# Conv taps released earlier, the local values projected behind the norm sums, compressed scores one head later

## The chip, the cores and the metric

The kernel runs on 1 core of one Trainium2 chip. The metric is the device time of one execution in microseconds (us). The engines are called TensorE (PE), VectorE (DVE), ScalarE (ACT), GpSimd (POOL) and SyncE (SP, which issues the loads). All matrix work is float32: a weight tile is split into a rounded part `hi` and a remainder `lo` by ACT and DVE, and PE makes three products of them.

## The reference, cut to what matters

Two transformer blocks follow each other on 256 tokens of width 1024. The change touches the second one, which computes, from `xn = rms_norm(x)`, three branches and their gated sum:

```python
q_nsa, kv_nsa, g_nsa, conv_in, q_mem, g_merge = split(xn @ w_in)
# branch 1: sparse attention, 8 heads: compressed scores, selected blocks, window
kc = rms_norm(compress_blocks(k_c));  vc = compress_blocks(v_c)
o_nsa = gate0 * softmax(q kc) vc + gate1 * softmax(q ks) vs + gate2 * softmax(q kw) vw
# branch 2: convolution of 31 taps over time, one weight per channel (512 channels)
u = a * sigmoid(ag)
u = silu(layer_norm(depthwise_conv(u, 31) + conv_b))
# branch 3: attention over 256 memory tokens, 4 heads
o_m = softmax(qm km) vm
gm = sigmoid(g_merge)
merged = gm[0] * (o_nsa @ w_nsa_out) + gm[1] * (u @ w_conv_out) + gm[2] * (o_m @ w_mem_out)
h = x + merged @ w_out            # then a gated feed-forward layer
```

## The kernel before, in words

Activations lie transposed: features on the 128 partitions, 256 tokens along the free axis. Weights stream in tiles of 128x1024; `Stream.prepare` issues the load on SP, the cast to `hi` on ACT (line 520) and the subtraction to `lo` on DVE (line 522), with 4 raw buffers and 3 each of `hi` and `lo`. A tile of the gate projection is 8 blocks of 128x128; its matmuls are 8 with `hi` (line 324), 8 with `hi` on the activation's remainder (line 326) and 8 with `lo` (line 328). Two tiles fill one PSUM buffer `pj`, and DVE takes it out into `gm` with line 1082.

Block two runs in these steps. The projection `w2a` makes the conv input `u`, the compressed operands, the heads' queries and keys. Then `compress` (a generator, stepped by `next(cmp)`) makes the compressed keys `kcn` and values, `nsa_operands` (stepped by `next(pre)`) makes the norm sums of queries and keys (line 1311, matmuls with 1 or 2 columns), their inverse roots `hn_y` and the split operands. `nsa` holds the attention: `first(n)` makes the scores of head n on PE, their maxima and the scaling on DVE and the exponentials on ACT; `scores()` makes the compressed scores of all heads, with a chain of 12 DVE steps on the tile `sc`; `turned(n)` transposes the weights of head n, `compressed()` transposes `sc` into `PcT` (line 1386), and `values(i)` multiplies with the values `vsw` and, as its last matmul, with `PcT` (line 1445). Between these steps stand the 24 tiles of the gate projection `w2g`, taken one at a time by `fill(gates, 1)`; they cover the attention's latency. `gemm_a` with `w2v` makes the local values `vsw` (line 367, 48 matmuls, two tiles).

What sets the order: from the heads' projection to the end of the gates PE's order is the written one (`manual_schedule` for PE alone). ACT, DVE and the rest of PE are ordered by a scheduler that takes the ready instruction of the highest priority; each engine then runs its queue strictly in order. Loads' splits and evacuations carry a raised priority. `issue_after(x)` keeps an instruction out of the queue until x stands in it.

The convolution is 4 columns of 31 DVE instructions on 128x256 (`conv_taps`, lines 1531 and 1534), each adding to `cv`. Columns 0 and 1 are free to go as soon as `u` is there. Column 2 is held until `N.marks[4]`, column 3 until `N.marks[7]`, where `N.marks[n]` is the product of gate and denominator of head n (line 1415). After the taps comes `conv_norm`: a fold on DVE (lines 1544, 1545), a mean matmul on PE (line 1549), the subtraction (line 1551), squares on ACT (line 1553), the sum matmul (line 396), an inverse root in small steps on DVE (lines 381 to 387), a transpose on PE that spreads it (line 403), the scaling (line 1560), a SiLU and the split into `uc`. Behind the gates PE runs the three output projections `wmo` (of `om`), `wno` (of `on`) and `wco` (of `uc`), then `wo2` (line 308 first).

Of the kernel before, what the change touches and what calls it, by code (L numbers as in the profile page):

```python
# [13 lines left out]
OP = mybir.AluOpType  # L14
# [423 lines left out]
def fill(steps, n):  # L438
    for _ in range(n):
        next(steps, None)  # L440


def finish(steps):
    for _ in steps:
        pass
# [93 lines left out]
def bc(ap, n, at=1):  # L539

    shape = list(ap.shape)
    shape.insert(at, n)
    return ap.unsqueeze(at).to_broadcast(shape)
# [499 lines left out]
def block_two(K, B, KM, vm, out):  # L1043
    nc, tc, a, par, con = K.nc, K.tc, K.a, K.par, K.con
# [7 lines left out]
    cv = K.t4("cv")  # L1052
    kc2 = [K.small("PT", [128, 384], bufs=4)[:, :256].rearrange("p (g t) -> p g t", g=2) for _ in range(2)]
    N = Bag()
# [3 lines left out]
    ag, u = K.t4("ag"), K.small("u", [128, 4, 286], bufs=1)  # L1058
# [39 lines left out]
    with tc.manual_schedule(engines={mybir.EngineType.PE}):  # L1098
        heads = K.steps_b(_Shift(st, 64), 8, 12, B.X, evb)
        fill(heads, 6)  # L1100
        cmp = compress(K, kc2, N)
        for _ in range(6):
            next(cmp)
            fill(heads, 1)
        next(cmp)
        pn = K.gemm_n(K.narrow("wgn", B.gain), B.x)
        with tc.high_priority(offset=50000):
            nc.vector.tensor_tensor(gn, pn, rr, op=OP.mult)
        next(cmp)
        K.gemm_a(K.stream("w2v", 256), 8, 1, B.X, 256, evv)  # L1110
        next(cmp)
        pre = nsa_operands(K, N, B.eps)
        next(pre)
        pg = K.pt()[:, :48].rearrange("p (t n) -> p t n", t=2)
        for t in range(2):
            mm(pg[:, t], lhsT=gn[:, t * 128:t * 128 + 128], rhs=con["fold"][:, :24], start=True, stop=True)
        N.gate = K.small("gate", [128, 2, 24], bufs=1)
        with tc.issue_after(s3.ins):
            nc.scalar.preload_act_table_set("natural_log_exp_and_others")
            sigmoid(K, N.gate, pg)  # L1120
        gates = K.steps_b(K.stream("w2g"), 8, 24, B.X, evg)
        fill(gates, 2)
        next(cmp)
        finish(pre)
        fill(gates, 1)
        finish(cmp)
        with tc.issue_after(s3.ins):
            last = nsa(K, N, ON, mem_attention(K, N, KM, vm, OM), gates)
        finish(gates)

    conv_taps(K, u, cv, {2: N.marks[4], 3: N.marks[7]})
    with tc.issue_after(last.ins):
        with tc.high_priority(offset=50000):
            UC = conv_norm(K, cv)
# [67 lines left out]
def compress(K, kc2, N):  # L1202

    nc, par, con = K.nc, K.par, K.con
    mm = nc.tensor.matmul
    pos = par["pos"].rearrange("p (k j) -> p k j", k=2)
    pa = K.pt().rearrange("p (k n) -> p k n", k=2)
    h = K.small("cmp_h", [128, 128], bufs=1)
    for kv in range(2):
        sides = []  # L1210
        for half in range(2):
            s = K.small("P0", [128, 2, 128], bufs=4).rearrange("p a (j c) -> p (a j) c", c=32)
            nc.gpsimd.memset(s[:, :, 30:], 0.0)
            with K.tc.high_priority(offset=50000):
                for g in range(2):
                    nc.vector.tensor_tensor(
                        s[:, :, g * 15:g * 15 + 15],
                        kc2[kv][:, g].rearrange("p (i j) -> p j i", j=8)[:, :, half:half + 15],
                        pos[:, kv, 8 * half:8 * half + 8].unsqueeze(2).to_broadcast([128, 8, 15]), op=OP.add)
            sides.append(s)  # L1220
        for ch in range(4):
            for j in range(4 * ch, 4 * ch + 4):
                if j % 2 == 0:
                    raw = K.small("P1", [128, 2, 256], bufs=4)
                    with K.tc.high_priority(offset=100000):
                        nc.sync.dma_start(raw, K.a["wc1"][kv * 4 + ch][:, (j % 4) * 256:(j % 4) * 256 + 512])
                o = 32 * (j % 4)
                mm(pa[o:o + 32, kv], lhsT=sides[j // 8][:, j % 8], rhs=raw[:, j % 2], start=j < 4, stop=j >= 12,
                   skip_group_check=True)
            if 4 * kv + ch < 7:  # L1230
                yield
    part = K.small("P1", [128, 2, 256], bufs=4)
    nc.scalar.copy(part, pa)
    yield
    ph = K.pt()[:, :128].rearrange("p (k m g c) -> p k m g c", k=2, m=2, g=2)
    for kv in range(2):
        for m in range(2):
            mm(ph[:, kv, m, :, :15], lhsT=part[:, kv, m * 128:m * 128 + 128],
               rhs=con["fold"], start=True, stop=True)
    hv = h.rearrange("p (a c) -> p a c", c=16)  # L1240
    phv = ph.rearrange("p k m g c -> p (k m g) c")
    nc.gpsimd.memset(h, 0.0)
    nc.vector.tensor_copy(hv[:, :, :15], phv[:, :, :15])
    t = K.small("cmp_t", [128, 128], bufs=1)
    nc.vector.tensor_tensor(t, h, h, op=OP.mult)
    nc.vector.tensor_scalar(t, t, 0.044715, 1.0, op0=OP.mult, op1=OP.add)
    nc.vector.tensor_tensor(t, t, h, op=OP.mult)
    sigmoid(K, t, t, 2 * (2 / np.pi) ** 0.5)
    nc.vector.tensor_tensor(h, h, t, op=OP.mult)
    yield  # L1250
    h5 = h.rearrange("p (k m c) -> p k m c", k=2, m=2)
    w2 = par["wc2"].rearrange("p (k m d) -> p k m d", k=2, m=2)

    pk = K.pt()[:, :16]
    for g in range(2):
        for m in range(2):
            mm(pk[g * 64:g * 64 + 64], lhsT=w2[:, 0, m], rhs=h5[:, 0, m, g * 16:g * 16 + 16], start=m == 0, stop=m == 1)
    k1, k2 = K.small("cmp_k", [128, 16], bufs=1), K.small("cmp_k2", [128, 16], bufs=1)
    nc.vector.tensor_copy(k1, pk)
    nc.vector.tensor_tensor(k2, k1, k1, op=OP.mult)  # L1260

    pv = K.pt()[:, :64]
    for i in range(4):
        for m in range(2):
            mm(pv[32 * i:32 * i + 32], lhsT=h5[:, 1, m], rhs=w2[:, 1, m], start=m == 0, stop=m == 1)
    N.vcb = K.small("cmp_v", [128, 128], bufs=1)
    nc.vector.tensor_tensor(N.vcb.rearrange("p (g d) -> p g d", g=2), bc(pv, 2),
                            con["slot"].unsqueeze(2).to_broadcast([128, 2, 64]), op=OP.mult)
    yield
    pn = K.pt()[:, :16]  # L1270
    mm(pn, lhsT=con["mean64"], rhs=k2, start=True, stop=True)
    nc.vector.tensor_scalar(k2, pn, EPS, None, op0=OP.add)
    y = rsqrt_exp(K, k2, *(K.small(n, [128, 16], bufs=1) for n in ("cmp_y", "cmp_w")))
    nc.vector.scalar_tensor_tensor(k1, k1, K.gain_k[:, 0:1], y, op0=OP.mult, op1=OP.mult)
    N.kcn = K.small("cmp_kn", [128, 2, 16], bufs=1)
    nc.vector.tensor_tensor(N.kcn, bc(k1, 2), con["half"].unsqueeze(2).to_broadcast([128, 2, 16]), op=OP.mult)


def sigmoid(K, out, x, scale=1.0):
# [66 lines left out]
def nsa(K, N, ON, mem, gates):  # L1346

    nc, par, con = K.nc, K.par, K.con
# [38 lines left out]


    cz = con["causal0"]
    S, N.marks = {}, {}  # L1390

    def first(n):
        i, g = divmod(n, 2)
# [55 lines left out]
    fill(gates, 1)  # L1449
    first(0)  # L1450
    fill(gates, 1)
    scores()
    first(1)
    fill(gates, 1)
    late = []
    for i in range(4):
        turned(2 * i)
        if i < 3:
            first(2 * i + 2)
        else:  # L1460
            late.append(mem(3))
            next(late[-1])
        fill(gates, 1)
        turned(2 * i + 1)
        if i == 0:
            compressed()
        fill(gates, 1)
        if i < 3:
            first(2 * i + 3)
        values(i)  # L1470
        fill(gates, 1)
        if i:
            next(late[-1 - (i == 3)])
        if i < 3:
            late.append(mem(i))
            next(late[-1])
        fill(gates, 1)
        if i:
            finish(late[-2])
        if i < 2:  # L1480
            fill(gates, 1)
# [42 lines left out]
def conv_taps(K, u, cv, behind):  # L1524
    nc, par, con = K.nc, K.par, K.con
    mm = nc.tensor.matmul
    w = par["conv_w"].rearrange("p (c k) -> p c k", c=4)
    for c in range(4):
        with K.tc.issue_after(behind[c].ins) if c in behind else nullcontext():
            o = cv[:, c * 256:c * 256 + 256]  # L1530
            nc.vector.tensor_scalar(o, u[:, c, :256], w[:, c, 0:1], par["conv_b"][:, c:c + 1],
                                    op0=OP.mult, op1=OP.add)
        for k in range(1, 31):
            nc.vector.scalar_tensor_tensor(o, u[:, c, k:k + 256], w[:, c, k:k + 1], o, op0=OP.mult, op1=OP.add)  # L1534
# [71 lines left out]
```

## Time and profile before

| | |
|---|---|
| times of three runs | 929.54, 930.87, 931.36 us (median 930.87) |
| the profiled execution | 931.74 us, of which the span is 929.9 us |
| PE busy | 903.5 us (97% of the span) |
| DVE busy | 680.2 us (73%) |
| ACT busy | 491.6 us (53%) |
| mean granted clock of PE | 0.987 of full speed |
| `lo` splits, DVE, line 522 | 278 of 1224 ns mean |
| conv taps, DVE, line 1534 | 120 of 476 ns mean |
| gate-like matmuls, PE, lines 324, 326, 328 | 280 to 300 ns each, every 120 ns at full clock |

The profile gives for each instruction its start, its duration and what its engine was waiting for. The durations of neighbours overlap (a matmul of 283 ns starts 120 ns after the last one), so costs below are differences of starts. A granted clock of 1.00 is TensorE's level of 2.4 GHz, 0.50 its level of 1.2 GHz. All windows are us from the start of the span; block two's part up to the output projection lies at 480 to 716.

### The profile page before, as it was taken

How to read it: one execution, taken by the hardware profiler on the slowest of the kernel's cores; microseconds unless marked ns; L12 is line 12 of the kernel's file. 1: busy time of each engine (PE TensorE's matmuls, PEld its weight loads, DVE VectorE, ACT ScalarE, POOL GpSimd, SP SyncE). 2: the span in 40 equal slices, each digit the busy share in tenths (PEclk: the TensorE clock that was granted, in tenths of full speed). 3: DMA queues.
4: the chain of work that ended last, by engine and by line, in shares of the span. 5: the costliest groups of instructions: out<-in, count | busy, mean ns of one | idle time of the engine just before them, and what ended most of it. 6: DMA issues, size and time to landing. Idle time of an engine off the chain costs nothing.

```text
span 929.9 us, 17029 instructions
## 1 busy us (share of the span) xinstructions
PE 903.5 (97%) x6818; PEld 831.3 (89%) x6818; DVE 680.2 (73%) x1169; ACT 491.6 (53%) x747; POOL 52.7 (6%) x82
## 2 busy tenths in 40 slices
PE   8998999999999999999999998999979999999998
PEld 6996789999999999888899897899869988888887
DVE  6997768866777665555567968789989788878653
ACT  6654665644556554444435435677734565555432
POOL 1000002200010000011110000000002200000000
PEclk9999999999999999999999979999989999999999
DMA  7644327665755666566655843244335556666662
GB/s 276 195 137 136 98 67 205 221 204 173 222 181 180 181 184 184 166 185 182 184 182 179 262 124 109 74 136 116 112 113 158 184 174 187 183 186 187 195 206 66
DMA packets 45728, 155.64 MB, mean 167 GB/s; under 512 B 5201, under 2 KB 6737, under 8 KB 45649
## 3 DMA queue, kind: packets, MB, share of 16 engines
q1 hardware_dynamic: 45216, 153.48, 54.1%
q8 instruction: 53, 0.87, 0.4%
q10 hardware_dynamic: 432, 1.08, 0.4%
q14 instruction: 27, 0.21, 0.1%
HBM read 153.49 MB, written 1.05 MB: 166 GB/s over the span
## 4 chain that ended last, share of the span: by engine, by line
PE 91%; DVE 5%; ACT 1%; issue 1%; DMA 0%; SPq 0%; DVEq 0%; ACTq 0%
PE pj L295 17%; PE pj L324 16%; PE pj L326 16%; PE pj L328 15%; PE pj L296 9%; PE pj L367 5%; DVE lo L522 2%; PE pj L309 1%; PE pj L310 1%; PE pj L308 1%; ACT hi L520 1%; PE pt L1311 1%; PE pt L913 1%; PE pt L1442 1%; PE pt L403 1%
## 5 line engine op out<-in xcount | busy, mean ns | idle before, releaser
L520 ACT CAST hi<-raw 128x1024 fp32r<-128x1024 f32 (+1 forms) x278 | 288.6, 1041 | 306.9 <-PE pj L326 139.2
L522 DVE TENSOR_TENSOR lo<-raw,hi 128x1024 fp32r<-128x1024 f32 (+1 forms) x278 | 339.8, 1224 | 105.2 <-ACT hi L520 97.2
L295 PE MATMUL pj<-hid,hi 128*128 128x512 f32 x378 | 134.2, 400 | 0.0
L295 PE MATMUL pj<-xf,hi 128*128 128x512 f32 x320 | 113.2, 399 | 0.0
L296 PE MATMUL pj<-hid,lo 128*128 128x256 f32 x378 | 106.2, 281 | 0.0
L296 PE MATMUL pj<-xf,lo 128*128 128x256 f32 x320 | 89.8, 281 | 0.0
L295 PEld LDWEIGHTS pj<-hid,hi 128*128 128x128 f32 x378 | 71.1, 188 | 17.3
L295 PEld LDWEIGHTS pj<-xf,hi 128*128 128x128 f32 x320 | 60.1, 188 | 14.9
L296 PEld LDWEIGHTS pj<-hid,lo 128*128 128x128 f32 x378 | 71.5, 189 | 0.0
L296 PEld LDWEIGHTS pj<-xf,lo 128*128 128x128 f32 x320 | 60.5, 189 | 0.0
L1534 DVE SCALAR_TENSOR_TENSOR cv<-u,par,cv 128x256 f32<-128x256 f32 x120 | 53.8, 476 | 1.2
L324 PE MATMUL pj<-xm,hi 128*128 128x256 f32 x336 | 52.1, 299 | 0.0
L324 PEld LDWEIGHTS pj<-xm,hi 128*128 128x128 f32 x336 | 45.7, 198 | 4.9 <-ACT hi L520 2.5
L326 PE MATMUL pj<-xm,hi 128*128 128x256 f32 x336 | 48.5, 288 | 0.0
L328 PE MATMUL pj<-xm,lo 128*128 128x256 f32 x336 | 47.2, 283 | 0.0
L469 POOL TENSOR_TENSOR acc<-acc,ffr 128x256 f32<-128x256 f32 (+1 forms) x25 | 27.3, 1101 | 310.9 <-ACT ffr L462 288.9
L328 PE MATMUL pj<-xn,lo 128*128 128x256 f32 x304 | 44.8, 286 | 0.0
L326 PEld LDWEIGHTS pj<-xm,hi 128*128 128x128 f32 x336 | 44.7, 198 | 0.0
L326 PE MATMUL pj<-xn,hi 128*128 128x256 f32 x304 | 44.0, 285 | 0.0
L324 PE MATMUL pj<-xn,hi 128*128 128x256 f32 x304 | 43.8, 285 | 0.0
L328 PEld LDWEIGHTS pj<-xm,lo 128*128 128x128 f32 x336 | 43.5, 193 | 0.0
L328 PEld LDWEIGHTS pj<-xn,lo 128*128 128x128 f32 x304 | 39.7, 192 | 0.5 <-issue 0.4
(471 smaller groups left out, 1639.0 us busy)
## 6 DMA issues: line engine op xcount, KB each, us to landing
raw<-in_wf_dram SPq DMA_DIRECT2D x64, 512.0 KB, 3.9
raw<-in_wgu_dram SPq DMA_DIRECT2D x44, 512.0 KB, 3.7
raw<-in_w1g_dram SPq DMA_DIRECT2D x24, 512.0 KB, 3.8
raw<-in_w2g_dram SPq DMA_DIRECT2D x24, 512.0 KB, 3.7
raw<-in_wdn_dram SPq DMA_DIRECT2D x22, 512.0 KB, 3.8
raw<-in_w2a_dram SPq DMA_DIRECT2D x20, 512.0 KB, 4.0
raw<-in_wo_dram SPq DMA_DIRECT2D x16, 512.0 KB, 3.7
raw<-in_w1a_dram SPq DMA_DIRECT2D x14, 512.0 KB, 4.5
```

What stands on the lines that cost most here:

```text
L295: mm(ps, lhsT=st.hi(w), rhs=x.both(k), start=k == 0, stop=False, skip_group_check=True)
L296: mm(ps[:, :T], lhsT=st.lo(w), rhs=x.h(k), start=False, stop=k == kt - 1, skip_group_check=True)
L308: mm(ps[:, j], lhsT=st.hi(w), rhs=x.h(k), start=k + j == 0, stop=False, skip_group_check=True)
L309: mm(ps[:, j], lhsT=st.hi(w), rhs=x.l(k), start=False, stop=False, skip_group_check=True)
L324: mm(ps[:, j], lhsT=st.hi(o + k), rhs=x.h(k), start=k == 0, stop=False)
L326: mm(ps[:, j], lhsT=st.hi(o + k), rhs=x.l(k), start=False, stop=False)
L328: mm(ps[:, j], lhsT=st.lo(o + k), rhs=x.h(k), start=False, stop=k == kt - 1)
L367: mm(pss[t], lhsT=xx(k)[:, t * 128:t * 128 + 128], rhs=ww(o + k), start=k == 0 and xx == x.h and ww == st.hi, stop=k == kt - 1 and ww == s ...
L469: self.engine.tensor_tensor(a, a, s, op=OP.add)
L520: nc.scalar.copy(hi[:, o:o + n], raw[:, o:o + n])
L522: nc.vector.tensor_tensor(lo[:, o:o + n], raw[:, o:o + n], hi[:, o:o + n].bitcast(F32), op=OP.subtract)
L1534: nc.vector.scalar_tensor_tensor(o, u[:, c, k:k + 256], w[:, c, k:k + 1], o, op0=OP.mult, op1=OP.add)
```

## The change

Three edits, all in block two:

1. The first two gate tiles are moved ahead, to where the values' projection stood, and `gemm_a` of `w2v` moves to where these tiles stood: behind the norm sums (line 1311), the transposes of the gate input and the gate's sigmoid, and ahead of the step of `compress` that needs its sigmoid.
2. `scores()` follows `first(1)` and no longer precedes it; and `compressed()` follows the gate tile that it preceded.
3. Column 2 of the conv is held until the compressed keys `kcn` are made, no longer until head 4; column 3 until head 4, no longer until head 7.

```diff
@@ block_two
-        K.gemm_a(K.stream("w2v", 256), 8, 1, B.X, 256, evv)
+        gates = K.steps_b(K.stream("w2g"), 8, 24, B.X, evg)
+        fill(gates, 2)
         next(cmp)
         pre = nsa_operands(K, N, B.eps)
         next(pre)
...
             sigmoid(K, N.gate, pg)
-        gates = K.steps_b(K.stream("w2g"), 8, 24, B.X, evg)
-        fill(gates, 2)
+
+        K.gemm_a(K.stream("w2v", 256), 8, 1, B.X, 256, evv)
         next(cmp)
...
-    conv_taps(K, u, cv, {2: N.marks[4], 3: N.marks[7]})
+    conv_taps(K, u, cv, {2: N.marks["keys"], 3: N.marks[4]})
@@ compress
-    nc.vector.tensor_tensor(N.kcn, bc(k1, 2), con["half"].unsqueeze(2).to_broadcast([128, 2, 16]), op=OP.mult)
+    N.marks = {}
+    N.marks["keys"] = nc.vector.tensor_tensor(N.kcn, bc(k1, 2), con["half"].unsqueeze(2).to_broadcast([128, 2, 16]), op=OP.mult)
@@ nsa
+    first(1)
     scores()
-    first(1)
     fill(gates, 1)
...
         turned(2 * i + 1)
+        fill(gates, 1)
         if i == 0:
             compressed()
-        fill(gates, 1)
```

No instruction's size or count of arithmetic changes. Lines behind the edits stand 1 or 2 lower in the changed file. How the queues move is shown at three places.

DVE, ahead of the inverse root `hn_y` that the compressed step on PE needs (`lo` is a weight tile's remainder, `gm` the evacuation of two gate tiles, `cmp_h` the compressed hidden layer). Before:

```order
L1284 RECIPROCAL gate_6162<-gate_6162 128x48
L522 TENSOR_TENSOR lo_6385<-raw_6382,hi_6384 128x1024
L1082 TENSOR_TENSOR gm_5244<-pj_6168,rr_5366 128x512
L1249 TENSOR_TENSOR cmp_h_5760<-cmp_h_5760,cmp_t_6113 128x128
L1294 SCALAR_TENSOR_TENSOR hn_y_6150<-hn_w_6151,hn_y_6150 128x32
```

and now:

```order
L1286 RECIPROCAL gate_6160<-gate_6160 128x48
L522 TENSOR_TENSOR lo_6385<-raw_6382,hi_6384 128x1024
L1250 TENSOR_TENSOR cmp_h_5760<-cmp_h_5760,cmp_t_6111 128x128
L1296 SCALAR_TENSOR_TENSOR hn_y_6148<-hn_w_6149,hn_y_6148 128x32
L1536 SCALAR_TENSOR_TENSOR cv_5250<-u_5257,par,cv_5250 128x256
```

The evacuation of the first two gate tiles has left this place; it now stands ahead of the norm sums.

DVE, at the end of the taps (`cv` the conv's sum, `ffr` its fold, `on` and `om` the attention outputs, `lo_7665` and later the tiles of `wmo`). Before:

```order
L1534 SCALAR_TENSOR_TENSOR cv_5250<-u_5257,par,cv_5250 128x256 x2
L1150 TENSOR_TENSOR gm_5249<-pj_7757,gm_5249 128x512
L522 TENSOR_TENSOR lo_7826<-raw_7823,hi_7825 128x1024
L1534 SCALAR_TENSOR_TENSOR cv_5250<-u_5257,par,cv_5250 128x256
L1544 TENSOR_TENSOR ffr_7586<-cv_5250 128x512
```

and now:

```order
L522 TENSOR_TENSOR lo_7665<-raw_7662,hi_7664 128x1024
L427 TENSOR_TENSOR on_5241<-pt_7363,on_5241 128x256
L1536 SCALAR_TENSOR_TENSOR cv_5250<-u_5257,par,cv_5250 128x256 x3
L1546 TENSOR_TENSOR ffr_7586<-cv_5250 128x512
L1547 TENSOR_TENSOR ffr_7586<-ffr_7586 128x256
L522 TENSOR_TENSOR lo_7697<-raw_7694,hi_7696 128x1024
L1082 TENSOR_TENSOR gm_5249<-pj_7375,rr_5366 128x512
L522 TENSOR_TENSOR lo_7729<-raw_7726,hi_7728 128x1024
L1553 TENSOR_TENSOR cv_5250<-cv_5250,pt_7587 128x1024
```

The taps end three instructions behind the last heads' `on`, ahead of the last gate evacuation; before, they ended among the evacuations of `wmo`, five weight tiles later.

PE, where the conv norm's inverse root is spread (line 403; `pj_7725` and `pj_7693` are pairs of `wmo`, `pj_7855` the fourth pair in the list `wmo`, `wno`). Before:

```order
L328 MATMUL pj_7855<-on_5241,lo_7859 128x256
L396 MATMUL pt_7596<-con,ffr_7586 128x1 x2
L328 MATMUL pj_7855<-on_5241,lo_7859 128x256
L403 MATMUL pt_7617<-con,rs_y_7604 128x128 x2
L324 MATMUL pj_7693<-om_5242,hi_7696 128x256 x2
```

and now:

```order
L326 MATMUL pj_7725<-om_5242,hi_7728 128x256 x2
L326 MATMUL pj_7725<-om_5243,hi_7728 128x256 x2
L328 MATMUL pj_7725<-om_5242,lo_7729 128x256 x2
L403 MATMUL pt_7617<-con,rs_y_7604 128x128 x2
L324 MATMUL pj_7693<-om_5242,hi_7696 128x256 x2
```

Between the sum (line 396) and the spreading (line 403) stood one matmul; now 33 of `wmo` stand there. The mean matmul (line 1549, now 1551) has moved from among `wno` to right behind the first memory-value product of the last head pair, ahead of all of `wmo`.

## Rows read from the trace of the kernel before

**Rows 1.** The page: the chain that ended last, shares of the span by engine.

```profile
PE 91%; DVE 5%; ACT 1%; issue 1%; DMA 0%; SPq 0%; DVEq 0%; ACTq 0%
```

**Rows 2.** Stretches: length, busy PE, PEld, DVE, ACT, POOL, granted clock, DMA share, GB/s.

```profile
547.00:553.00 6.00, 6.00 (x32) 6.00 (x31) 0.00 (x0) 0.00 (x0) 0.00 (x0) 0.53 0.31 87
561.40:564.00 2.60, 0.05 (x1) 0.00 (x0) 2.21 (x6) 0.18 (x1) 0.00 (x0) 1.00 0.48 172
564.00:568.40 4.40, 4.34 (x48) 3.84 (x49) 3.06 (x11) 0.41 (x1) 0.00 (x0) 0.61 0.43 123
577.00:579.20 2.20, 0.17 (x3) 0.03 (x1) 2.20 (x9) 0.88 (x2) 0.00 (x0) 1.00 0.50 188
581.00:585.30 4.30, 4.30 (x24) 4.12 (x24) 3.46 (x18) 0.94 (x3) 0.00 (x0) 0.60 0.12 48
579.40:598.90 19.50, 18.32 (x132) 16.14 (x131) 14.17 (x57) 13.88 (x38) 0.00 (x0) 0.91 0.29 82
598.90:615.00 16.10, 16.10 (x131) 15.86 (x131) 10.60 (x33) 12.17 (x31) 0.00 (x0) 1.00 0.44 132
615.00:665.00 50.00, 50.00 (x399) 46.12 (x398) 48.38 (x130) 37.67 (x79) 0.00 (x0) 1.00 0.41 118
665.00:715.60 50.60, 42.59 (x311) 40.46 (x311) 44.92 (x76) 20.12 (x28) 8.69 (x4) 0.93 0.39 124
686.80:691.80 5.00, 0.00 (x0) 0.00 (x0) 4.62 (x14) 0.14 (x1) 2.08 (x1) 0.89 0.35 126
691.80:697.40 5.60, 5.59 (x26) 5.60 (x27) 4.04 (x9) 3.05 (x6) 0.00 (x0) 0.50 0.00 0
```

**Rows 3.** Waits, 530 to 720: who waited for whom, total us, times, longest.

```profile
PE pt L403 <- DVE rs_y L387: 5.0, 1, 5.0
...
PE pt L1257 <- DVE hn_y L1294: 2.6, 1, 2.6
...
PE pt L1364 <- DVE cmp_kn L1276: 2.0, 1, 2.0
```

**Rows 4.** Timeline of DVE behind the norm sums: start, us, instruction.

```profile
561.89 1.22 DVE L522 TENSOR_TENSOR lo<-raw,hi 128x1024 fp32r<-128x1024 f32 x1 [0.40 <-ACT hi L520]
563.04 0.68 DVE L1082 TENSOR_TENSOR gm<-pj,rr 128x512 f32<-128x512 f32 x1
563.64 0.28 DVE L1249 TENSOR_TENSOR cmp_h<-cmp_h,cmp_t 128x128 f32<-128x128 f32 x1
563.84 0.18 DVE L1294 SCALAR_TENSOR_TENSOR hn_y<-hn_w,hn_y 128x32 f32<-128x32 f32 x1
```

**Rows 5.** Timeline of DVE at the compressed scores.

```profile
578.93 0.19 DVE L1276 TENSOR_TENSOR cmp_kn<-cmp_k,con 128x32 f32<-128x32 f32 x1
...
593.39 0.42 DVE L1386 COPY PcT<-pt 128x256 f32<-128x256 f32 x1 [0.30 <-PE pt L1385]
```

**Rows 6.** Timeline of PE at the compressed scores.

```profile
580.97 1.23 PE L1398 MATMUL pt<-ks,qs 128*128 128x256 f32 x4
...
598.31 0.69 PE L1445 MATMUL pt<-PcT,cmp_v 32*128 32x256 f32 x2
```

**Rows 7.** Timeline of DVE at the last conv taps.

```profile
659.43 0.42 DVE L427 TENSOR_TENSOR on<-pt,on 128x256 fp32r<-128x256 f32 x1
659.76 2.56 DVE L1534 SCALAR_TENSOR_TENSOR cv<-u,par,cv 128x256 f32<-128x256 f32 x5
...
679.22 0.48 DVE L1534 SCALAR_TENSOR_TENSOR cv<-u,par,cv 128x256 f32<-128x256 f32 x1
```

**Rows 8.** Timeline of PE from the last gates to the output projection.

```profile
665.07 1.03 PE L1518 MATMUL pt<-PTm,vm 128*128 128x256 f32 x4
...
681.01 0.70 PE L1549 MATMUL pt<-ffr,con 128*128 128x256 f32 x2
...
691.81 0.69 PE L403 MATMUL pt<-con,rs_y 128*128 128x128 f32 x2 [5.03 <-DVE rs_y L387]
...
715.58 0.28 PE L308 MATMUL pj<-mrg,hi 128*128 128x256 f32 x1
```

More of the change, by code (lines that the diff above doesn't have):

```diff
@@ L1389, in nsa @@
     cz = con["causal0"]
-    S, N.marks = {}, {}
+    S = {}
     def first(n):
```

## The prediction

> **What bounds the kernel now.** I read the page first. Its chain of waits gives PE 91% and DVE 5% [rows 1], and the table gives PE 97% busy: the time is PE's queue, and it shortens where PE waits or runs at half clock. The stretches show where that is in block two [rows 2]. From 598.9 to 665 PE is busy 66.1 of 66.1 us at a granted clock of 1.00; nothing is to be had there. The losses lie at three places, and the list of waits names their releasers [rows 3]:
>
> - 561.4 to 564.0: PE is busy 0.05 us; it waits 2.6 us for `hn_y`. Then 4.4 us run at a clock of 0.61.
> - 577.0 to 579.2: busy 0.17 us; it waits 2.0 us for `cmp_kn`, the tile of `kcn`. From 581.0 to 585.3 the clock is 0.60.
> - 665 to 715.6: busy 42.59 of 50.60 us, so 8.0 us idle, 5.0 of them at line 403 for `rs_y`. Behind it 5.6 us run at 0.50, which costs 5.6 x 0.50 = 2.8 us. Together 10.8 us.
>
> **Edit 1, the gate tiles ahead of the norm sums.** PE's work is only swapped: `gemm_a` and the two gate tiles have 48 matmuls each, 0.12 us apart. What shortens the wait for `hn_y` is DVE's queue. Before `hn_y` stand there the split `lo` (561.89), `gm` (563.04), `cmp_h` (563.64) and `hn_y` itself (563.84) [rows 4]. The evacuation `gm` leaves this place, as the order shows: 563.64 - 563.04 = 0.60 us. What starts DVE's run there, the cast on ACT that `lo` waits for (0.40 us), is as it was, and it gives 0 or 0.40. So the gain is 0 (if `hn_y`'s own chain through ACT ends last) to 1.0, and up to 1.4 with a little of the 4.4 us at 0.61 back. I take 0.8: the evacuation is a direct row, the rest a fraction. The loads of the two weights change places in SP's queue and are of the same size; four raw buffers let them be issued ahead, so I count nothing for them. If that cover were gone, a tile late by its split would cost one `lo`, 1.22 us.
>
> On the half clock behind the two waits, a row and a rule part. From 547 to 553 PE is busy 6.00 of 6.00 us, without a wait, and is granted 0.53 [rows 2]: matmuls of one and two columns keep the clock down there by themselves. The Trainium skill, "TensorE: Matmul & The Clock Gate", section "Loop structure matters more than you think", says that the loop nest decides whether matmuls stay warm, and that waits between them send the clock down. By that rule the half clock behind each of the two waits would go with the wait; by the row it may stay. I let most of it stay.
>
> **Edit 2, scores one head later.** The 4 matmuls of a head's scores are busy 1.23 us at the nearest row [rows 6], and the last one's end overlaps what follows, so that I count 1.0. They now stand ahead of the wait for `kcn` and fill 1.0 of its 2.0 us. That is the gain, unless the head's queries are late themselves (0). If the wait's end also spares half clock, 4.3 x 0.40 = 1.7 us come on top: 0 to 2.7.
>
> The same edit has a price. `scores()` brings 12 DVE steps on `sc`, which end in the copy to `PcT`. Before, they run at once; now the reductions of head 1 and a few taps that edit 3 sets free come first. From `cmp_kn` (578.93) to the copy (593.39) it was 14.5 us [rows 5], in a window where DVE is busy 14.17 of 19.5 us [rows 2]. The foreign work ahead of it is now about 6 taps (6 x 0.51 = 3.1 us) and the head's reductions (some 1.5), of which part falls into the 5.3 idle us: I estimate 16 us, so the copy ends at about 595.4 if `cmp_kn` comes as before. The first reader on PE is line 1445 at 598.31 [rows 6], 2.9 us later. A front gain of 2.2 leaves 0.7 of that, so PE does not wait, or by up to 2 us. I take 1.4 for edit 2: the 1.0, and 0.4 of the half clock. Bounds: -1 (all cover gone) to 2.7. Front together: 2.2, from 0 to about 4.
>
> **Edit 3, the taps.** Before, `on` of the last heads is at 659.43, five taps follow at 659.76 (2.56 us, 0.51 each), and the last of the 22 taps behind `on` is at 679.22 [rows 7]; between them stand splits and evacuations of `wmo`. By the order three taps now follow `on`. So 19 taps, 19 x 0.51 = 9.7 us, must go into DVE's idle time earlier. There is 5.3 us in 579.4 to 598.9, 5.5 in 598.9 to 615, and 50.0 - 48.38 = 1.6 in 615 to 665 [rows 2], together 12.4 us, less the 2.2 that the front gains: 10.2 us. It fits, with 0.5 us over, and then DVE is full. Since an ordered queue does not use every gap, I let the fold end between 661.5 and 667. PE comes to the mean matmul behind the last gate and the first memory values, at 665.07 plus 0.5 less the front's 2.2, so at 663 to 664 [rows 8]: cover for most of that range.
>
> From the mean matmul (681.01) to line 403 (691.81) it took 10.8 us, and PE had only one matmul between the sum and line 403 [rows 8]. Now 45 matmuls of `wmo` stand between the mean and line 403, 45 x 0.12 = 5.4 us, and some 1.8 us of memory values, their sums and the conv's sum: 7.2 us. The chain of the norm on DVE is about as long as before: DVE was busy 4.62 of the last 5.0 us of it [rows 2], and by the order three splits and an evacuation of others still lie among its steps. So 10.8 - 7.2 = 3.6 us of wait would be left, less what waits for `om` in the same time; I take 3.0 us in all. The two columns of `wmo` and `wno` behind it (over 150 matmuls) cover the SiLU and the split `uc`. With PE waiting 3 us in two pieces, I take the half clock as gone. Gain of edit 3: 10.8 - 3.0 = **7.8**; bounds 2.8 (the fold 5 us late, which PE waits out at the mean) to 10.8 (no wait and no half clock left). That is between far ends; I choose near the upper one because the nearest row, 666 as PE's arrival against an end of the taps at 661 to 667, has PE last.
>
> The middle, 598.9 to 665, I cost at nothing: the same matmuls, and DVE's splits of the gate tiles can run two tiles ahead of PE with three buffers. A tile is 24 matmuls, 2.9 us of PE, so the cover is some 5.8 us against a `lo` of 1.22. If that cover is gone, each tile costs what DVE lags.
>
> **Sum.** The profiled execution took 931.74 us; 931.74 - 0.8 - 1.4 - 7.8 = 921.7. It lies 0.87 above the median of 930.87, so the forecast against the median is **920.9 us**.
>
> **Rivals.**
>
> 1. The front gains nothing: `PcT` or the half clock takes back what the waits gave. 931.74 - 7.8 - 0.87 = 923.1. For it speaks the row at 0.53 without a wait; against it the `gm` that has left the queue. 0.17.
> 2. DVE is full and the fold comes 5 us late: PE waits at the mean matmul, with line 403's 3.0 as well. 931.74 - 2.2 - 2.8 - 0.87 = 925.9. For it: only 0.5 us of idle DVE time is left over. 0.13.
> 3. All waits go and no half clock remains: 4.0 at the front and 10.8 behind, 916.1. For it: 150 matmuls are to be had as cover; against it the chain of 10.8 us over 7.2. 0.14.
> 4. Nothing measurable: PE's work is the same, and 930.9 stays. Against it the order, in which the taps do move. 0.03. The Trainium skill, "Perfetto Trace Analysis", section "Identifying the Most-Contended Engine", advises to work at the engine that is contended most; PE's work does not fall here. By that rule this rival would hold; the 8.0 idle us of the tail speak against it.
> 5. Slower. Taps stand ahead of the splits of gate tiles, and DVE falls behind by more than its lead of 5.8 us. From that point each later tile waits: with 0.8 us (an estimate: two thirds of a `lo`) over 16 tiles that is 12.8 us, less the 10.0, so 931.74 + 2.8 - 0.87 = 933.7. Against it: 9.7 us of taps have 10.2 us of room, so DVE would have to lose some 6 us to badly placed waits first. 0.03.
>
> **How the numbers follow.** The forecast has 0.50. A measurement of this kernel can tell about 0.2%, 1.9 us, from no change. The forecast and rivals 1 to 3 are all faster by more: 0.94; rival 4 is same, 0.03; rival 5 slower, 0.03. The range reaches from below rival 3 to above rival 2: 915.5 to 926.5. It leaves out rivals 4 and 5 and some spread about rivals 2 and 3, about 0.15.
>
> **What would show it.** Edit 1: the wait for `hn_y` is 1.6 to 2.0 us, no longer 2.6. Edit 2: the wait for `cmp_kn` is under 1.2 us and line 1447 (1445 before) waits for `PcT` under 1 us. Edit 3: the last tap starts by 665, the mean matmul does not wait, PE waits 1 to 2 us at line 403 and is granted 0.9 or more in the 6 us behind it. From the last gate to the first matmul of `wo2` it is 41 to 44 us instead of 50.5. Wrong I would be most if DVE ended the taps after 668, or if gate tiles between 600 and 665 waited for `lo`.

## The result and the profile after

The changed kernel took 918.43 us (median; 916.09 to 920.02) against 930.73 us before: a ratio of 0.9877, with an interval of 0.9850 to 0.9905. Measured a second time, beside other kernels, it was 917.84 us and 0.9857 (0.9835 to 0.9879). The forecast was 920.9 us in a range of 915.5 to 926.5. By the medians 12.3 us were gained where 10.0 were forecast; by the ratio, which is not the quotient of the two medians (0.9868), it is 11.4.

The profiled execution of the changed kernel took 920.02 us with a span of 918.2. Its chain of waits, against [rows 1]:

```profile
PE 94%; DVE 3%; issue 1%; ACT 1%; DMA 0%; SPq 0%; DVEq 0%
```

The list of PE's waits from the norm sums to the output projection (engine, tile and line that waited, releaser, us in total, times, longest), against [rows 3]:

```profile
PE pt L1258 <- DVE hn_y L1296: 2.0, 1, 2.0
PE pt L1430 <- DVE P L1420: 1.1, 1, 1.1
PE pt L1520 <- DVE om L427: 0.8, 1, 0.8
PE pt L1400 <- ACT ks L1345: 0.7, 1, 0.7
PE pj L324 <- ACT om L426: 0.5, 1, 0.5
PE pt L1366 <- DVE nb L1411: 0.5, 1, 0.5
PE pt L1430 <- ACT P L1419: 0.4, 1, 0.4
PE pt L1447 <- DVE PcT L1388: 0.2, 1, 0.2
```

Line 403 has left the list: its 5.0 us are gone, and so is the half clock behind it. The wait for `hn_y` is 2.0 us, no longer 2.6. The wait for `cmp_kn` is 0.5, and 0.7 for a piece of `ks` stand ahead of it. At the transposes of the weights (line 1430) the kernel before waited 0.48 us at head 0 and 0.48 + 0.22 us at head 1; now it is 0.44 + 1.12 us at head 0 and nothing at head 1. The 1.12 us are new.

The stretches (length, busy PE, PEld, DVE, ACT, POOL, granted clock, DMA share, GB/s), against [rows 2]:

```profile
553.20:562.50 9.30, 9.30 (x53) 9.17 (x53) 4.86 (x16) 2.47 (x6) 0.00 (x0) 0.65 0.08 16
564.70:569.00 4.30, 4.30 (x61) 4.01 (x61) 3.99 (x12) 1.54 (x3) 0.00 (x0) 1.00 0.35 122
597.70:615.00 17.30, 17.30 (x141) 17.10 (x141) 16.67 (x50) 13.02 (x32) 0.00 (x0) 1.00 0.41 122
615.00:664.80 49.80, 49.80 (x394) 45.76 (x392) 46.89 (x125) 37.13 (x79) 0.00 (x0) 1.00 0.41 122
664.80:703.80 39.00, 37.63 (x305) 36.60 (x304) 34.59 (x59) 19.27 (x27) 7.04 (x4) 1.00 0.50 156
```

From 597.7 to 664.8 PE is busy throughout, as before. In the tail it is idle for 39.00 - 37.63 = 1.37 us, 1.30 of them in the two waits for `om`, at full clock. DVE, at 10.60 of 16.1 us before, is now busy 16.67 of 17.3 behind the first values: the taps went there.

The tail in detail, the timelines of DVE and then of PE (start, us, instruction), against [rows 7] and [rows 8]:

```profile
658.23 0.42 DVE L427 TENSOR_TENSOR on<-pt,on 128x256 fp32r<-128x256 f32 x1
658.56 1.51 DVE L1536 SCALAR_TENSOR_TENSOR cv<-u,par,cv 128x256 f32<-128x256 f32 x3
660.18 0.69 DVE L1546 TENSOR_TENSOR ffr<-cv 128x512 f32<-128x512 f32 x1
660.91 0.43 DVE L1547 TENSOR_TENSOR ffr<-ffr 128x256 f32<-128x256 f32 x1
```

```profile
663.82 1.03 PE L1520 MATMUL pt<-PTm,vm 128*128 128x256 f32 x4
...
664.80 0.60 PE L1551 MATMUL pt<-ffr,con 128*128 128x256 f32 x2
...
667.46 1.10 PE L1520 MATMUL pt<-PTm,vm 128*128 128x256 f32 x4 [0.84 <-DVE om L427]
669.02 0.38 PE L324 MATMUL pj<-om,hi 128*128 128x256 f32 x1 [0.46 <-ACT om L426]
...
669.96 0.50 PE L396 MATMUL pt<-con,ffr 128*128 128x1 f32 x4
...
674.58 0.40 PE L403 MATMUL pt<-con,rs_y 128*128 128x128 f32 x2
...
703.85 0.28 PE L308 MATMUL pj<-mrg,hi 128*128 128x256 f32 x1
```

The fold is done at 661.34, and PE comes to the mean at 664.80: 3.5 us of slack. From there to line 403 it is 9.8 us, 1.3 of them waits for `om`, and no wait is listed at line 403. From the last gates' memory values (663.82) to the first matmul of `wo2` (703.85) it is 40.03 us, against 715.58 - 665.07 = 50.51 before.

### The profile page after: what moved, and what is told of

Read it like the earlier page. It is cut to its first block, busy times and chain, and to the rows that moved or that the text cites. A ratio compares the mean times of both kernels' runs of the same rounds, so it can differ in the third digit from the quotient of the medians.

```text
span 918.2 us, 17035 instructions
## 1 busy us (share of the span) xinstructions
PE 900.6 (98%) x6818; PEld 828.4 (90%) x6818; DVE 675.6 (74%) x1169; ACT 491.1 (53%) x747; POOL 51.1 (6%) x82
## 4 chain that ended last, share of the span: by engine, by line
PE 94%; DVE 3%; issue 1%; ACT 1%; DMA 0%; SPq 0%; DVEq 0%
PE pj L295 18%; PE pj L324 17%; PE pj L326 16%; PE pj L328 16%; PE pj L296 9%; PE pj L367 6%; DVE lo L522 1%; PE pj L309 1%; PE pj L310 1%; PE pj L308 1%; ACT hi L520 1%; PE pt L913 1%; PE pt L1313 1%; PE pt L403 1%; PE pt L1229 1%
## 5 line engine op out<-in xcount | busy, mean ns | idle before, releaser
L324 PEld LDWEIGHTS pj<-xm,hi 128*128 128x128 f32 x336 | 44.2, 193 | 5.0 <-ACT hi L520 2.5
L326 PEld LDWEIGHTS pj<-xm,hi 128*128 128x128 f32 x336 | 44.1, 195 | 0.0
```

What stands on the lines that cost most here:

```text
L324: mm(ps[:, j], lhsT=st.hi(o + k), rhs=x.h(k), start=k == 0, stop=False)
L326: mm(ps[:, j], lhsT=st.hi(o + k), rhs=x.l(k), start=False, stop=False)
```

## The experiments

Two lengths are read from each profile. The **front** runs from the first norm-sum matmul to the first product with `PcT`; the **tail** from the last gates' memory values to the first matmul of `wo2`. Between them no wait of PE is listed, whatever the kernel. "Waits" is the sum of PE's waits in the front. The front of before begins at 545.80 and ends at 598.31 ([rows 6]); the front of the changed kernel is read from the second pair of lines:

```profile
545.80 7.29 PE L1311 MATMUL pt<-con,hsq 128*128 128x2 f32 x40
```

```profile
547.01 6.38 PE L1313 MATMUL pt<-con,hsq 128*128 128x2 f32 x40
...
597.06 0.69 PE L1447 MATMUL pt<-PcT,cmp_v 32*128 32x256 f32 x2 [0.22 <-DVE PcT L1388]
```

Front and tail come from one execution of each kernel, the medians from all of its runs; the two need not add up. The medians of before in the three rounds of measurements were 930.72, 930.71 and 931.35 us.

| kernel | median us | ratio (interval) | front | waits in it | tail |
|---|---|---|---|---|---|
| before | 930.7 | 1 | 52.51 | 5.83 | 50.51 |
| edit 1 | 933.03 | 1.0022 (1.0002 to 1.0042) | 51.97 | 6.95 | 50.52 |
| edit 2 | 929.13 | 0.9984 (0.9968 to 1.0000) | 48.76 | 5.34 | 50.34 |
| edit 3 | 925.03 | 0.9932 (0.9910 to 0.9955) | 56.16 | 7.90 | 40.03 |
| edits 1, 2 | 927.65 | 0.9956 (0.9939 to 0.9972) | 49.72 | 4.74 | 49.51 |
| edits 1, 3 | 921.93 | 0.9921 (0.9899 to 0.9944) | 52.41 | 7.43 | 40.03 |
| edits 2, 3 | 918.99 | 0.9888 (0.9866 to 0.9909) | 48.99 | 5.61 | 40.03 |
| all three | 918.43 | 0.9877 (0.9850 to 0.9905) | 50.05 | 4.96 | 40.03 |
| all three, again | 917.84 | 0.9857 (0.9835 to 0.9879) | 50.11 | 4.96 | 40.01 |
| column 3 at head 6 | 918.85 | 0.9879 (0.9855 to 0.9903) | 48.43 | 4.87 | 40.66 |
| column 3 at head 7 | 922.48 | 0.9901 (0.9876 to 0.9926) | 50.11 | 4.96 | 42.82 |
| `compressed()` early | 920.70 | 0.9888 (0.9866 to 0.9910) | 52.23 | 6.92 | 40.03 |

**Each edit alone.** Edit 1 and edit 2 are the hunks of the diff above, each applied to the kernel before by itself; edit 3 alone is

```diff
-    nc.vector.tensor_tensor(N.kcn, ...
+    N.marks = {}
+    N.marks["keys"] = nc.vector.tensor_tensor(N.kcn, ...
...
-    conv_taps(K, u, cv, {2: N.marks[4], 3: N.marks[7]})
+    conv_taps(K, u, cv, {2: N.marks["keys"], 3: N.marks[4]})
```

> Edit 1 alone: the first two gate tiles ahead of the norm sums, the values' projection behind them; the scores, the compressed step and the taps as before. Against 930.7 us before. The prediction's term: 0.8 us, so 929.9. The trace of after: from the first norm sum to the first gate tile behind the compressed step it is 1.8 us shorter (566.98 - 545.80 = 21.18 before, 566.39 - 547.01 = 19.38 after), so 928.9. Rival, that this is a chance of the clock in one execution: within 0.3 us of before.

> Edit 2 alone: compressed scores behind the second head's scores, their transposition one gate tile later; taps and values as before. The prediction's term: 1.4 us, so 929.3. The trace of after: from the first gate tile behind the compressed step to the one behind the first values it is 31.96 before and 31.29 after, 0.7 us, so 930.0: the 1.0 us won at the keys is mostly given back in two waits at the transposes of head 0 (0.44 and 1.12 us). Rival: all is given back, or more, 930.7 to 931.5.

> Edit 3 alone: column 2 of the conv held until the compressed keys, column 3 until head 4; the values and scores as before. The prediction's term: 7.8 us, so 922.9. The trace of after: from the last gates' memory values to the output projection 50.51 before and 39.98 after, 10.5 us, so 920.2, if the tail's gain needs nothing of the front. Rival, that the tail's gain leans on the front's edits: without them PE comes to the chain's transposes earlier against DVE, taps delay them, and 2 us or more are lost, 922.5 to 925.

Edit 1 alone came out slower, by an interval that just clears 1 (1.0002), which no theory here had expected. PE's waits show a part of it:

```profile
PE pt L1429 <- DVE P L1419: 2.1, 1, 2.1
...
PE pt L1258 <- DVE hn_y L1295: 2.0, 1, 2.0
```

The wait for `hn_y` did shrink from 2.62 to 2.02, by the very 0.60 of the evacuation. But at the transposes of head 1 PE now waits 2.1 us for the weights `P`; it was 0.48 there. On DVE, just ahead of those weights:

```profile
588.23 1.23 DVE L522 TENSOR_TENSOR lo<-raw,hi 128x1024 fp32r<-128x1024 f32 x1 [0.37 <-ACT hi L520]
589.37 0.17 DVE L1415 RECIPROCAL den<-den 128x4 f32<-128x4 f32 x1
...
589.77 0.48 DVE L1419 TENSOR_SCALAR P<-P,den 128x128 f32<-128x128 f32 x2
```

A weight's split stands ahead of `den` and `P`. In the kernel before it stood behind them:

```profile
591.34 0.48 DVE L1418 TENSOR_SCALAR P<-P,den 128x128 f32<-128x128 f32 x2
591.86 1.23 DVE L522 TENSOR_TENSOR lo<-raw,hi 128x1024 fp32r<-128x1024 f32 x1
```

All waits of the front together grew by 1.1 us (5.83 to 6.95), half of the 2.3 by the medians. Where the other half comes from is not shown; in its profiled execution the front of this kernel is even 0.5 us shorter than before, since the clock differed (below). With edit 3 alone it is the same place, with 3.0 us:

```profile
PE pt L1429 <- DVE P L1419: 3.0, 1, 3.0
```

```profile
592.19 0.47 DVE L1535 SCALAR_TENSOR_TENSOR cv<-u,par,cv 128x256 f32<-128x256 f32 x1
592.58 1.22 DVE L522 TENSOR_TENSOR lo<-raw,hi 128x1024 fp32r<-128x1024 f32 x1
...
593.80 0.45 DVE L1535 SCALAR_TENSOR_TENSOR cv<-u,par,cv 128x256 f32<-128x256 f32 x1
...
594.29 0.49 DVE L1535 SCALAR_TENSOR_TENSOR cv<-u,par,cv 128x256 f32<-128x256 f32 x1
594.70 0.48 DVE L1419 TENSOR_SCALAR P<-P,den 128x128 f32<-128x128 f32 x2
```

Three freed taps and a split precede `P`. The front is 3.65 us longer than before (56.16 against 52.51), 2.07 of them waits (7.90 against 5.83) and the other 1.58 the same matmuls at a lower clock, while the tail has the whole gain: 50.51 - 40.03 = 10.5. So the rival held for the front, the theory for the tail, and the median of 925.03 lies at the upper end of the rival's 922.5 to 925. Edit 2 alone came out at 929.13, within 0.2 us of the prediction's term, but its interval reaches 1.0000.

**The pairs.**

> Edits 1 and 2 without the taps' earlier release. The prediction: 0.8 + 1.4 = 2.2 us, so 928.5, if the terms add. The trace of after: 2.5 us, so 928.2. Rival, that the front's gain is swallowed at the end: the taps of before end with DVE, not with PE; if DVE's queue sets the last tap (679.22) and not PE, an earlier front buys nothing there, and it is 930 to 930.7.

> Edits 2 and 3, the values' projection where it was before. Theory, that edits 2 and 3 need each other: with edit 3 alone PE waited 3.04 us at the transposes of head 1 for `P` from DVE (line 1419 there), because taps and the split stood ahead of head 1's weights; edit 2 makes these scores ahead of the keys, so that this wait goes. Then the tail's 10.5 us and most of edit 2's own gain stay: 918 to 920. Rival, the prediction's sum of independent terms, 1.4 + 7.8 = 9.2: 921.5; or by the medians of the single edits, 1.6 + 5.7 = 7.3: 923.4, with a wait of 3 us left at the transposes of head 1.

> Edits 1 and 3, the scores and the compressed step as before. Theory, that edit 2 is what lets the other two pass: both put DVE work ahead of head 1's weights (a wait of 2.14 us there with edit 1 alone, of 3.04 with edit 3 alone), so PE waits 3 us or more at the transposes of head 1, and it is 925 to 928, no faster than edit 3 alone (925.0). Rival, the prediction's independent terms, 0.8 + 7.8: 922.1.

Edits 1 and 2 gave 3.1 us by the medians, though one alone cost 2.3 and the other gave 1.6. The waits of the front go the same way: +1.1 and -0.5 us alone, -1.1 together. With head 1's scores a gate tile's time earlier, the 2.1 us at head 1 are gone, and at head 0 there are 1.3 us for `P` from DVE where edit 2 alone has 1.1. The rival, that DVE's end of the taps swallows a gain of the front, fell. Edits 2 and 3 gave all but what the measurement cannot tell apart (918.99 against 918.43 and 917.84). Edits 1 and 3 kept the wait at head 1:

```profile
PE pt L1430 <- DVE P L1420: 3.0, 1, 3.0
```

Here the theory had the place and size of the wait (3 us or more) and missed the time: 921.93, where the rival's sum had 922.1. Its figure was added from medians which the clock of the front disturbs (below), and the rival's is luck, since its sum has no such wait: against edit 3 alone only 0.5 us of wait went (7.90 to 7.43), and the medians lie 3.1 us apart. Tails are the same to 0.1 us in all four kernels with edit 3, so what the pairs tell of the front is that edit 2 is the one that counts there: with edit 3, it takes the waits from 7.90 to 5.61 us. Beside edits 2 and 3, edit 1 shows 0.65 us less of wait (5.61 to 4.96), and by the times it cannot be told from nothing, since the intervals overlap.

**The second half of edit 2.**

```diff
         turned(2 * i + 1)
-        fill(gates, 1)
         if i == 0:
             compressed()
+        fill(gates, 1)
```

> The changed kernel without the second half of edit 2: the transposition of `sc` stands ahead of the gate tile again, as before. In the changed kernel `sc` is ready at 593.62 and PE is behind the transposes of head 1 at 591.35. Theory, that the move is needed since the chain of `sc` now runs later: PE waits 2.0 to 2.5 us there, 920.5. Rival, that the wait at the first values (0.22) and at the transposes goes in exchange, or the scheduler puts the chain ahead of taps: within 0.5 us, 918.5.

```profile
PE pt L1387 <- DVE den L1416: 2.2, 1, 2.2
```

The theory held in place, size and time: 2.2 us at the transposition of `sc`, 920.7 us. The halves of edit 2 need each other as well: what comes a head later must also be read a tile later.

**How early the taps must be free.** The changed kernel with column 3 held longer:

```diff
-    conv_taps(K, u, cv, {2: N.marks["keys"], 3: N.marks[4]})
+    conv_taps(K, u, cv, {2: N.marks["keys"], 3: N.marks[6]})
```

> The changed kernel with column 3 of the conv held until head 6, no longer head 4. By its order 11 taps follow the last heads' `on`, not 3, among two splits and one evacuation, and the mean matmul stands 16 matmuls of `wmo` later. Theory, that the place of the taps alone sets the tail: 8 taps x 0.5 = 4 us and the two splits, 2.4, make the fold some 6 us later; 3.5 of them are slack (fold done at 661.3, PE at the mean at 664.8), so 1.5 to 4 us are lost in the tail, 920 to 922.5, and the wait at line 403 is back with 1 to 4 us. Rival, that the front gave DVE enough room and the hold no longer matters: within 0.5 us of the changed kernel, 918.5.

and the same with `N.marks[7]`:

> The changed kernel with column 3 held until head 7 as before, column 2 free at the compressed keys: half of edit 3. By the order 17 taps follow the last `on` (before 22, with head 6 11, changed 3). With head 6 the tail was 40.66 us against 40.03, since PE was given `wmo` matmuls ahead of a later mean. Theory now, that slack and these matmuls cover a fold that is late by some 4 us and no more: 6 taps more make it 3 to 5 us later still, line 403 waits 1 to 4 us again, and it is 920.5 to 924. Rival, that DVE's work before 660 matters and not its place: the tail stays within 1 us, 918 to 919.5.

With head 6 the theory fell: 8 more taps behind the last `on` cost 0.6 us of tail, 918.85 us. With head 7 the time, 922.48, is in the theory's range, but not the mechanism: line 403 does not wait there either. The tail is 2.8 us longer than the changed kernel's; 1.2 of them are waits (2.46 against 1.30), and these lie elsewhere:

```profile
PE pj L328 <- DVE lo L522: 1.1, 2, 0.7
...
PE pj L324 <- ACT om L426: 0.8, 2, 0.5
```

The mean comes 12.0 us behind the memory values, not far from the 15.9 of the kernel before, and yet nothing is lost at the norm:

```profile
675.94 0.70 PE L1551 MATMUL pt<-ffr,con 128*128 128x256 f32 x2
...
680.98 0.50 PE L396 MATMUL pt<-con,ffr 128*128 128x1 f32 x4
...
685.67 0.43 PE L403 MATMUL pt<-con,rs_y 128*128 128x128 f32 x2
```

What differs is where mean and sum stand in PE's order. Between the sum (line 396) and line 403 stand, counted in the orders of the kernels, 1 matmul of `wmo` and `wno` before, 24 with head 7, 46 with head 6, 33 in the changed kernel. Line 403 itself has hardly moved with head 7: of the 192 matmuls of `wmo` and `wno`, 119 stand ahead of it and 73 behind, where before it was 120 and 72. But 68 of them stand ahead of the mean, where before it was 93. So with head 7 PE has other work while DVE makes the inverse root, 4.69 us from the sum to line 403; before, it had one matmul for 5.76 us and waited 5.0:

```profile
686.05 0.50 PE L396 MATMUL pt<-con,ffr 128*128 128x1 f32 x4
```

Half of edit 3, the earlier release of column 2, thus wins 7.7 of the tail's 10.5 us (50.51 to 42.82). The 72 matmuls behind line 403, 72 x 0.12 = 8.6 us, could have run in the wait of before: `om` and `on` were long finished, and the last split of their weights began at 687.42. A kernel with the taps of before and only line 403 moved back was not tried. It could not have won everything, as an estimate from these rows: PE would have come to `uc` at some 695.8 (line 403 at 691.8 less 5.0, plus 8.6 and 0.4), and the last piece of `uc` was made at 704.7, so waits would have come up there.

One part of the wait of before has another cause. The first step of the inverse root on DVE, an instruction on 128x2, took 1.23 us there; it ends together with an addition on POOL:

```profile
687.68 2.08 POOL L1152 TENSOR_TENSOR gm<-gm,gm 128x512 f32<-128x512 f32 x1 [211.87 <-DVE gm L1150]
```

```profile
688.56 1.23 DVE L381 TENSOR_SCALAR rs_i<-rms_v 128x2 int32<-128x2 int32 x1
```

In the changed kernel the addition comes later (689.41) and the same step takes 0.17 us:

```profile
670.69 0.17 DVE L381 TENSOR_SCALAR rs_i<-rms_v 128x2 int32<-128x2 int32 x1
```

So it is in all profiles: 1.23 us in the four kernels without edit 3, 0.16 to 0.17 us in all with it or a part of it. Some 1.1 of the 5.0 us are this.

**One step further.** The changed kernel still waits 2.0 us for `hn_y`. One gate tile more there, taken from the second pair of heads, with column 3 free at head 2 so that the taps find room:

```diff
         K.gemm_a(K.stream("w2v", 256), 8, 1, B.X, 256, evv)
+        fill(gates, 1)
         next(cmp)
...
-        if i < 2:
+        if i < 1:
             fill(gates, 1)
...
-    conv_taps(K, u, cv, {2: N.marks["keys"], 3: N.marks[4]})
+    conv_taps(K, u, cv, {2: N.marks["keys"], 3: N.marks[2]})
```

> An attempt at more: the changed kernel with one more gate tile between the values' projection and the compressed step (it covers the 2.02 us wait for `hn_y`), taken from the second pair of heads, and column 3 of the conv held until head 2. Theory: PE does 2.9 us of gate tile in the wait, which goes, and the later tiles have enough cover: 2.0 us less, 916.4, and up to 1.5 more if less half clock follows. Rival: the tile's remainder `lo` (563.02 in the changed kernel, ahead of `hn_y`) keeps `hn_y` where it is relative to the tile, or the second pair's transposes wait 2 us for want of the tile: 918 to 920.

It took 915.35 us, 0.9839 (0.9814 to 0.9864), 1 us below the theory's figure; the interval overlaps that of the changed kernel. In the profile the wait for `hn_y` is gone and the waits of the front are 2.83 us, no longer 4.96; of them 0.55 lie at the new tile and 2.1 at the keys, where the changed kernel waited 0.46:

```profile
PE pt L1367 <- DVE nb L1412: 2.1, 1, 2.1
```

The tail is the changed kernel's (40.02 us), so the earlier release of column 3 shows nothing there.

Then a second tile, from the first pair of heads to ahead of `first(1)`:

```diff
     first(0)
-    fill(gates, 1)
+    fill(gates, 2)
     first(1)
```

(with the `fill` under `if i < 1` taken out).

> A further step from v1_m2: a second gate tile moved forward, from the first pair of heads to ahead of the second head's scores, where v1_m2 still waits 2.06 us for the keys. Theory: the tile of 2.9 us covers that wait, 2 us less than v1_m2: 913.4. Rival: `kcn` stands behind the tile's split and evacuation on DVE (1.15 and 0.6 us) and moves with it, so most of the wait stays: 914.5 to 916; or the first heads' transposes and values now wait for want of the tile, 916 to 918.

914.12 us, 0.9824 (0.9800 to 0.9847): in the same round of measurements the changed kernel had 917.84, and its fastest run (916.66) is slower than the slowest of this one (916.50). The wait at the keys went, as the theory had it, but 2.4 us came up at the next place, the transposition of `sc`, as the second rival had in kind. Over the kernel with one tile moved no gain is shown: the runs of the two overlap, and the waits of the front are 3.26 us, no fewer than 2.83:

```profile
PE pt L1388 <- DVE den L1418: 2.4, 1, 2.4
```

**The clock of the front.**

> The changed kernel once more, beside the three others on one chip. Both readings of the noise expect a median of 917.5 to 919.5. What its profile tells apart: if the half clock of the front is set by the kernel's own order, its places and its loss are those of the first profile (561 at 0.5 to 0.7, then 580 to 584 at 0.57; first norm sum to first `PcT` product 50.05 us); if it falls by chance, they differ, by 1 us or more, with the same waits.

The waits were the same to 0.03 us, the places of the half clock not. The same two stretches, behind the wait for `hn_y` and behind that for the keys, in the first execution of the changed kernel and then in the second (columns as above):

```profile
564.50:570.00 5.50, 5.41 (x70) 5.15 (x71) 5.05 (x16) 2.52 (x4) 0.00 (x0) 1.00 0.28 95
578.30:584.50 6.20, 6.19 (x40) 6.20 (x41) 3.38 (x20) 3.46 (x11) 0.00 (x0) 0.72 0.27 87
```

```profile
564.50:570.00 5.50, 5.50 (x39) 5.17 (x37) 3.64 (x10) 2.50 (x4) 0.00 (x0) 0.69 0.21 82
578.30:584.50 6.20, 5.44 (x43) 5.00 (x43) 4.64 (x22) 4.83 (x14) 0.00 (x0) 1.00 0.24 87
```

In the first execution the clock is whole behind the wait for `hn_y` and low behind the one for the keys; in the second it is the other way round. The front's length was equal all the same, 50.05 and 50.11. The expectation that chance would show as a difference of 1 us was not met by this pair. Front less waits, which is the same matmuls in every kernel up to the changes of order, ran from 43.4 us (edit 2; edits 2 and 3) over 45.1 (changed) to 48.3 (edit 3); the kernel with column 3 at head 6, whose front is that of the changed kernel, had 43.6. So 1.5 us and more of a front's length come and go with the clock in one and the same order of PE, and a single profile cannot give an edit's gain there. How much of the spread between kernels of different order is chance was not measured.

## Why the prediction was right, and where it was off

**What bounds the kernel** was right: PE's queue, at three places, with nothing to gain between 598.9 and 665. The whole gain is in front and tail: 2.46 + 10.48 = 12.9 us between the two profiled executions, less 1.2 lost ahead of the front, where 931.74 - 920.02 = 11.7 were measured.

**Edit 1.** The step from the row of `gm` to a wait shorter by 0.60 us held exactly, in every kernel with this edit that still waits there (2.02 against 2.62). The 0.8 us as a gain did not hold: what a split does that is pushed ahead of the weights of head 1 was not looked for, and alone the edit lost 0.2% (0.02 to 0.42%). The step that failed is that only the queue ahead of `hn_y` was read, and not that ahead of the next thing that PE waits for. The half clock was rightly not promised with the wait: in the changed kernel 553.2 to 562.5 ran at 0.65 without a wait and 564.7 to 569.0 at 1.00 behind one. The Trainium skill, "TensorE: Matmul & The Clock Gate", "Loop structure matters more than you think", speaks of a "long DMA wait between every matmul"; the prediction stretched that to single waits of 2.6 and 2.0 us for DVE, and in these traces such a wait does not settle the clock behind it.

**Edit 2.** The wait at the keys went to 0.46 + 0.70 us, near the "1.0 of 2.0" filled, and `PcT` is waited for by 0.22 us, within the "by up to 2 us"; its copy came 18.6 us behind `cmp_kn` (577.98 to 596.59), not the 16 of the estimate. The term was taken as independent, 1.4 us. The pairs show that its worth depends on the others: with edit 3 it gives 6 us by the medians (925.03 to 918.99). Of these 2.3 are waits (7.90 to 5.61), above all the 3.0 at head 1; the profiles have the rest in the clock of the front, whose matmuls took 48.3 us without edit 2 and 43.4 with it, and that it would be so in every execution is not shown. The prediction had no row of the weights of head 1 in it; the wait at head 0 that the edit itself makes (1.12 us) was not foreseen either.

**Edit 3** was the mis-sized term: 7.8 forecast, 10.5 measured in the tail, in four profiles alike. The taps fitted, as worked out, with more room than the 0.5 us reckoned: the fold was done at 661.34, just ahead of the forecast's 661.5 to 667. The prediction had PE arrive at 663 to 664 in one place and at 666 in another; it came to the mean at 664.80. The step that failed is the 3.0 us of wait left over, 10.8 us of chain less 7.2 of cover. The chain was taken to be as long as before and took 9.6 us (`rs_y` is there at 674.43), 1.1 us less by the one DVE step that POOL's addition no longer lengthens. The cover was 8.5 us of work and not 7.2, with 46 matmuls of `wmo` in it where 45 were counted. With the two waits for `om` PE needs 9.8 us from the mean to line 403, so nothing is left there, and 1.3 us of wait in all stand in place of the 3.0. That is 1.7 of the missing 2.7 us. The other 1.0 is PE's busy time in the tail: it fell from 42.51 to 38.66 us, by 3.85, where the half clock had been priced at 2.8; which matmuls make the difference was not looked into. Two of the prediction's signs failed with this step: the 1 to 2 us at line 403, and the 41 to 44 us from the last gate to `wo2`, which are 40.03. The matmuls behind line 403 were put at over 150; 146 stand there.

**The sum** is 2.5 us too high (920.9 against 918.43), about what edit 3 was short of (7.8 against 10.5). The front looks like a hit, 2.2 us forecast against 2.5 in the two profiles (52.51 to 50.05), and that is luck: its waits fell by 0.87 us only (5.83 to 4.96), and the other 1.6 are matmuls at a higher clock, which come and go between executions of one kernel. In the profiled execution 1.4 us went the other way by the clock, in block one where the kernels are the same (below). Rivals 2 and 5, DVE too full, fell for the changed kernel; the mechanism of rival 5, taps ahead of what PE waits for, appeared where edit 2 was missing, at one place and not at every tile. Rival 1, a front that gains nothing, fell with edits 1 and 2 together (0.9939 to 0.9972). Rival 3 held for the tail (10.5 of its 10.8 us) and not for the waits of the front. Rival 4 fell, and with it what was drawn from the Trainium skill, "Perfetto Trace Analysis", "Identifying the Most-Contended Engine": PE's work is unchanged, and its idle time and half clock were worth 12 us. The advice itself, to optimize the most-contended engine first, is not refuted by that: the gain was found on PE, in its waits.

## What to carry to other kernels

When a strictly ordered engine waits, look at what stands behind the waiting instruction in its queue: here 8.6 us of ready work did. Once the taps ended earlier, the sum stood 24 to 46 matmuls ahead of line 403 and the wait was gone; moving the waiting instruction alone was not tried. Price moved work at every consumer that it passes, not only at the one it is moved for; a split or a few taps ahead of one head's weights made waits of 2.1 and 3.0 us. Edits that were made together should be measured apart and in pairs before their terms are added: here +2.3 and -1.6 us made -3.1, by medians that are known to some 2 us.

## What the hardware showed that was not expected

The granted clock differs between executions where the kernel is the same. In block one, which no edit touches, the changed kernel's profiled execution lost 1.4 us (the same matmuls of line 367 start at 90.03 before and at 91.47 then); the stretch of before first, then of the changed kernel:

```profile
76.00:90.00 14.00, 12.76 (x81) 10.05 (x82) 9.10 (x14) 7.87 (x12) 0.00 (x0) 1.00 0.48 147
```

```profile
76.00:90.00 14.00, 12.95 (x75) 9.99 (x76) 7.65 (x12) 7.45 (x12) 0.00 (x0) 0.88 0.50 148
```

14.0 x (1.00 - 0.88) = 1.7 us of full clock are missing there; the first norm sum of block two starts 1.2 us later than before. The runs of one kernel spread by 2 to 9 us (925.98 to 933.47 for the kernel before); whether the clock makes all of that spread was not measured. Therefore effects under 1 us were here read from waits in the profiles and not from times.

Also not expected was the DVE step of 1.23 us, 0.17 elsewhere, that ended with POOL's addition (both above). A split on DVE that began 0.26 us ahead of that addition (687.42) took its usual 1.22 us beside it; why the one instruction was held up and the other not, no run here shows.
